# Routing of a top-2-of-8 expert layer: rows normed by products with a diagonal matrix and a row of ones, counts and registers in another order, gates in a function called from the product loop

## The chip, the cores and the metric

The program runs on one core of a Trainium2 chip. The metric is the device time of one execution in microseconds (us), the median of several runs. The core's engines are TensorE (PE in the rows, with its weight loads as PEld), VectorE (DVE), ScalarE (ACT), GpSimd (POOL) and SyncE (SP), each with its own queue of instructions that it works off in order. TensorE's clock has two levels, 1.2 and 2.4 GHz; the rows give the granted clock as a share of the upper one.

## The reference: what is computed

Two layers over 512 latent tokens of width 1024 with a context prefix of 256 tokens. Each layer is a norm, a projection, four groups of mixers, an output projection, and then a norm and a feed-forward part. The change is in the feed-forward part of the second layer, eight experts of which each token uses two:

```
h      = rms_norm(x) modulated: h = (x * rstd) * A + B, A and B vectors over the 1024 channels
logits = h @ router                       # 512 x 8
top 2 experts of each token; gates = softmax over the two logits
y      = sum over the two of gate * (silu(h @ w1) * (h @ w3)) @ w2     # 1408 hidden units per expert
out    = rms_norm(x + g2 * y)
```

All operands are float32.

## The kernel before, in words

Products with weights are made in three passes (`mm3`, lines 272 to 274): each operand is split into a high and a low part that the array multiplies exactly, the high part by a ScalarE copy (L259), the low part by a VectorE subtraction (L260). `load_split` issues the load of a weight tile on SP's queue into a tile named `raw...` and then splits it into `hi...` and `lo...`.

`moe_x` turns each of the eight channel tiles of the residual so that tokens are on partitions, and leaves `x A` in `hm`, a tile of 128 partitions by 4 blocks of 1024 channels. `moe_route` then does the following, in this order of the text:

- It sums the squares on TensorE (L1658) and takes `rs`, the reciprocal root mean square (tile `mrs`), and the logits `lg` of each token.
- It norms the rows: ScalarE multiplies each block of `hm` by `rs` (L1671), GpSimd adds `B` (tile `Br`) to three of the four blocks (L1673), VectorE to the last one (L1700). Four DMAs on ScalarE's queue write them to a DRAM buffer `hd` (L1702).
- It ranks the eight logits of each token by comparing all pairs on VectorE (`rank`, L1680 to L1684), selects the two best (`one`, `sel`), and computes the gates.
- It counts the tokens of each expert, and each token's position, by eight small products with triangular matrices and matrices of ones (L1708 to L1712), copies both out of the accumulator (`pos`, L1714), and ranks the experts by their counts.
- The numbers of the experts in that order go to `regs` (L1730), which SP loads into registers; the addresses of the weight loads depend on them. Everything else (some 40 small VectorE instructions) leads to `inv` (L1774), the token of every row of the dispatch buffer, which comes out of eight products with one-hot matrices (L1773).

`moe_run` then walks eight runs of experts: three of two blocks of 128 rows and five of one block, in two lanes that take turns. GpSimd's queue gathers the rows of a block from `hd` by `inv` (`xr`, L1799), TensorE turns them (L1812), ScalarE and VectorE split them (`xh`, `xl`). For each of eleven tiles of hidden units of a run two loads (`rawm`, three buffers) and one (`rawv`, two buffers) come in; the first product goes into `sml`, then Silu (`mt`, L1840), then the second product into `y`.

The order in which the instructions of an engine stand is not that of the text: a scheduler writes it out ahead of the run from the dependences, and the engines keep to it. Tiles that are allocated in the pool `mh` (of the routing) give their room to tiles of the product loop; tiles in `mo` live to the end.

Of the kernel before, what the change touches and what calls it, by code (L numbers as in the profile page):

```python
# [23 lines left out]
T = LAT + CTX  # L24
# [10 lines left out]
# columns of the per-layer parameter block  # L35
# [4 lines left out]
# columns of the constant block  # L40
# [7 lines left out]
def _consts():  # L48
    """Constants that depend on shapes alone."""
# [54 lines left out]
def _col_tiles():  # L104
    """Column tiles (lists of w_in columns) that are computed channels x tokens, and the token-major group."""
# [17 lines left out]
# heads 0, 2, 1, 3  # L123
# [6 lines left out]
def _pack(inp):  # L130
# [7 lines left out]
    # shifts and scales of two channel tiles side by side  # L138
# [84 lines left out]
class Ker:  # L223
# [19 lines left out]
    def weave(*gens):  # L243
        """Traces several streams side by side: (generator, steps at a time)."""
# [31 lines left out]
    def gemm_col(s, ps, parts, act, segs):  # L276
        """ps[:, tokens] = weights^T act for one tile of 128 output channels.  parts: (first k, tiles) of the weights."""
# [53 lines left out]
    def seg_gemm(s, lhsT, rhs, ntok, use, tag=None):  # L331
        """use(columns, psum) for each segment of lhsT^T rhs; lists of operands are summed."""
# [46 lines left out]
    def setup_masks(s):  # L379
        """The constants that the recurrences need."""  # L380
# [7 lines left out]
        # masks of the pairs that hold the diagonal as well  # L388
# [31 lines left out]
    def ada_rest(s, tp, room):  # L420
        """The first layer's second half and the second layer, a channel tile at a time, without the tensor engine.
        s.adaw(): where the weights of a tile go."""
# [4 lines left out]
        for n in range(72):  # L427
# [4 lines left out]
            # the second layer's context goes no further than its keys  # L432
# [12 lines left out]
    def sumsq(s, m, n, pool, x=None, eng=None):  # L445
        """Adds the squares of channel tile m of the residual to s.acc."""
# [31 lines left out]
    def norm(s, l, mod, sh, sc, gcol, wp, rs, hhi, hlo, ks, ts=None):  # L478
        """Channel tiles ks of the normalised and modulated residual in two parts; ts: room for two tiles."""
# [18 lines left out]
    def proj(s, l, cols, eng=None):  # L498
        """Column tiles (number, tokens) of the input projection into PSUM (channels x tokens); several at once go k by k."""
# [4 lines left out]
    def proj_tok(s, l, it, vt):  # L504
        """HGRN inputs and window values, tokens on partitions."""
# [39 lines left out]
    def rw_prep(s, l, last, g, tp):  # L545
        """Everything of the RWKV mixer that needs no state."""
# [34 lines left out]
        # values, centred over the channels of their head, tokens on partitions  # L581
# [9 lines left out]
        # bonus: (sum over the head of r k r_k) v  # L591
# [17 lines left out]
    def flip(s, out, lhs, rhs, start=True, stop=True):  # L609
        """out[half j] = lhs(j)^T rhs(j) for both j; the array's column halves work side by side."""  # L610
# [11 lines left out]
    def rw_first(s, last, g, tp):  # L622
        """The first operands of the first direction, ahead of the rest."""
# [43 lines left out]
        # the chain of a pair beside the operands of the next  # L667
# [17 lines left out]
    def rw_pair(s, d, lo, last, g, tp, z):  # L685
        """Operands and triangular inverses of two neighbouring chunks of one direction."""
# [34 lines left out]
        # G^T = [-beta|kappa]^T [alpha|rho], masked  # L721
# [9 lines left out]
        # (I + L)^-1 by doubling.  T: the inverses (TU, padded TP), TT: their transposes  # L731
# [15 lines left out]
        # kappa and -beta, tokens on partitions  # L747
# [12 lines left out]
        for i in range(1, 6):  # L760
# [4 lines left out]
            def half(x):  # L765
                # the columns of the earlier half of every block
# [28 lines left out]
    def rw_chain(s, d, lo, ch, last, g, O, done, tp, z, ops, Z, final):  # L795
        """One chunk of the state recurrence; returns the state after it."""
# [44 lines left out]
    def head_squares(s, O, i, a, b, sq):  # L841
        """Sums of squares of the heads of chunks a .. b of recurrence i's output."""
# [3 lines left out]
    def head_rms(s, last):  # L846
        """Their reciprocal root means."""
# [41 lines left out]
    def hg_gates(s, l, z, key, tp, tmp):  # L889
        """log decays (cumulated within the chunks, in z) and keys of both directions."""  # L890
# [25 lines left out]
        # log max(f, 1e-30) as the sum of two logarithms whose arguments stay in the range of the function  # L916
# [11 lines left out]
    def hgrn(s, last, q, b, key, it, O, tp):  # L928
        """The recurrences of both directions, in segments of four chunks."""
# [13 lines left out]
        def padded(dst, f, sel, engs):  # L943
            """dst[half, c, t, half, sel] = f(half)"""
# [4 lines left out]
        for d in range(2):  # L949
# [3 lines left out]
            for sg in ((2, 1, 0) if d else (2, 0, 1)):  # L953
# [3 lines left out]
                # keys scaled to the end of their chunk, tokens on partitions  # L957
# [1013 lines left out]
```

## Time and profile before

| | us |
|---|---|
| median of 3 runs | 2638.28 |
| lowest and highest run | 2634.31, 2647.7 |
| span of the profiled execution, first to last instruction | 2644.5 |
| TensorE busy in the span | 2408.1 |
| VectorE busy | 1660.6 |
| ScalarE busy | 1227.3 |
| GpSimd busy | 484.9 |

The page gives the profiled execution only its span. Of the three runs only the one of 2647.7 us is longer than that span, by 3.2 us, so this is the one that the span fits into, and 3.2 us would lie around it. Times in rows are counted from the span's start. The last products of the layer's output projection end at about 2019 us, the routing follows, and the product loop of the experts runs from about 2050 to about 2602 us.

### The profile page before, as it was taken

To read this page: it belongs to the slowest core of one execution; us is meant where nothing else is said; L and a number is where in the kernel's file an instruction comes from. 1 tells how busy PE (TensorE), PEld (TensorE's weight loads), DVE (VectorE), ACT (ScalarE), POOL (GpSimd) and SP (SyncE) were. 2 spreads that over 40 slices of the span, in tenths; PEclk is the share of its full clock that TensorE was granted. 3 is DMA by queue.
4 is the path that set the end of the run, shared out by engine and by line. 5 is a ranking of instruction groups with operands and counts; after the bars stand their busy time and mean duration, and the time that the engine had idled before them with its cause. 6 is when DMAs were issued, how large, how long until landed. Compare 5 with 4: busy or idle time off the path is not lost. (4 is left out here: it accounts for less than half of the span.)

```text
span 2644.5 us, 46379 instructions
## 1 busy us (share of the span) xinstructions
PE 2408.1 (91%) x18131; PEld 1998.6 (76%) x18131; DVE 1660.6 (63%) x3055; ACT 1227.3 (46%) x2331; POOL 484.9 (18%) x613
## 2 busy tenths in 40 slices
PE   6999788879998999999999997888996999999994
PEld 3889666656586888888888786666674898899993
DVE  5573598777578644344336746876745667667765
ACT  4373356546723211211234654664653556555653
POOL 1010464441011000000020005654102000000002
PEclk9999899989998999999999998998998899999997
DMA  6223110111053433334322130001113888888885
GB/s 245 65 89 111 49 34 20 30 65 57 1 178 129 144 112 120 117 116 132 118 81 64 57 116 13 20 16 49 56 36 107 267 270 270 280 265 264 260 277 179
DMA packets 161026, 322.46 MB, mean 122 GB/s; under 512 B 12288, under 2 KB 84736, under 8 KB 160800
## 3 DMA queue, kind: packets, MB, share of 16 engines
q1 hardware_dynamic: 153744, 293.60, 34.2%
q0 software_dynamic: 6480, 23.73, 2.5%
q8 instruction: 144, 2.36, 0.4%
q10 hardware_dynamic: 576, 2.10, 0.2%
q14 instruction: 82, 0.67, 0.1%
HBM read 295.39 MB, written 22.54 MB: 120 GB/s over the span
## 5 line engine op out<-in xcount | busy, mean ns | idle before, releaser
L272 PE MATMUL big<-hhi,hiw 128*128 128x512 f32 (+1 forms) x1504 | 520.8, 347 | 9.1 <-ACT hhi L491 4.6
L273 PE MATMUL big<-hlo,hiw 128*128 128x512 f32 (+1 forms) x1504 | 523.6, 348 | 2.4 <-DVE hlo L492 2.4
L274 PE MATMUL big<-hhi,low 128*128 128x512 f32 (+1 forms) x1504 | 519.5, 346 | 5.8 <-DVE low L260 3.9
L259 ACT CAST hiw<-raww 128x512 fp32r<-128x512 f32 (+3 forms) x208 | 158.4, 769 | 616.9 <-PE big L273 413.4
L272 PEld LDWEIGHTS big<-hhi,hiw 128*128 128x128 f32 x1504 | 286.2, 191 | 53.2 <-ACT hhi L491 5.7
L274 PEld LDWEIGHTS big<-hhi,low 128*128 128x128 f32 x1504 | 286.2, 190 | 45.1 <-DVE low L260 5.6
L273 PEld LDWEIGHTS big<-hlo,hiw 128*128 128x128 f32 x1504 | 286.4, 190 | 41.0 <-DVE hlo L492 4.2
L260 DVE TENSOR_TENSOR lom<-rawm,him 128x1024 fp32r<-128x1024 f32 x176 | 215.1, 1225 | 128.0 <-ACT him L259 126.7
L260 DVE TENSOR_TENSOR low<-raww,hiw 128x512 fp32r<-128x512 f32 (+3 forms) x196 | 177.3, 909 | 161.1 <-ACT hiw L259 160.8
L259 ACT CAST him<-rawm 128x1024 fp32r<-128x1024 f32 x176 | 184.3, 1047 | 150.4 <-PE sml L273 60.7
L272 PE MATMUL sml<-xh,him 128*128 128x256 f32 x528 | 152.0, 288 | 0.0
L273 PE MATMUL sml<-xl,him 128*128 128x256 f32 x528 | 149.5, 283 | 0.0
L274 PE MATMUL sml<-xh,lom 128*128 128x256 f32 x528 | 149.4, 283 | 0.0
L260 DVE TENSOR_TENSOR lov<-rawv,hiv 128x1024 fp32r<-128x1024 f32 x88 | 107.5, 1222 | 38.2 <-ACT hiv L259 37.8
L272 PE MATMUL sml<-him,xh 128*128 128x256 f32 x440 | 127.4, 290 | 0.7 <-DVE xl L260 0.6
L273 PE MATMUL sml<-lom,xh 128*128 128x256 f32 x440 | 125.4, 285 | 0.0
L274 PE MATMUL sml<-him,xl 128*128 128x256 f32 x440 | 125.3, 285 | 0.0
L273 PE MATMUL big<-gl,hiw 128*128 128x512 f32 (+1 forms) x352 | 119.5, 339 | 0.0
L272 PE MATMUL big<-gh,hiw 128*128 128x512 f32 (+1 forms) x352 | 118.9, 338 | 0.0
L274 PE MATMUL big<-gh,low 128*128 128x512 f32 (+1 forms) x352 | 118.2, 336 | 0.0
L259 ACT CAST hiv<-rawv 128x1024 fp32r<-128x1024 f32 x88 | 92.4, 1050 | 51.3 <-PE y L274 41.5
L757 POOL TENSOR_TENSOR Gm<-G,mskf 128x256 f32<-128x256 f32 x120 | 99.5, 836 | 85.7 <-PE a L612 82.5
(560 smaller groups left out, 5633.7 us busy)
## 6 DMA issues: line engine op xcount, KB each, us to landing
rawm<-in_m SPq DMA_DIRECT2D x176, 512.0 KB, 5.1
rawv<-in_m SPq DMA_DIRECT2D x88, 512.0 KB, 4.7
raww<-in_wadt SPq DMA_DIRECT2D x56, 512.0 KB, 3.5
raww<-in_w SPq DMA_DIRECT2D x52, 512.0 KB, 3.9
raww<-in_winc SPq DMA_DIRECT2D x92, 256.0 KB, 2.8
raww<-in_wout SPq DMA_DIRECT2D x16, 512.0 KB, 4.1
wadt<-in_wadt SPq DMA_DIRECT2D x16, 512.0 KB, 4.4
raww<-in_w SPq DMA_DIRECT2D x16, 448.0 KB, 3.3
```

Source lines behind the costliest of these rows:

```text
L259: s.S.copy(hi, src)
L260: (eng or s.V).tensor_sub(lo, src, hi)
L272: s.E.matmul(out, ah, bh, start=start, stop=False)
L273: s.E.matmul(out, ah, bl, start=False, stop=False)
L274: s.E.matmul(out, al, bh, start=False, stop=stop)
L757: P.tensor_mul(x, G[:, :, 0, :, 0], s.mskf[:, 1 - d, i][:, None, None].to_broadcast(sh))
```

## The change

It edits `moe_route`, moves part of it into a new function `moe_tables`, and passes that function to `moe_run`, which calls it behind its third step.

- **Rows.** For each of the four blocks of `hm` ScalarE writes a diagonal matrix `dg` (the unit matrix with each row scaled by `rs`). For each half of 512 columns TensorE multiplies `hm` by it and adds, by a product of a row of ones with `Br`, the vector B to each token's row, in an accumulator `ph` of the three buffers `tx`; ScalarE copies that back to `hm`. The block's DMA to `hd` follows. The operands are plain float32.
- **Selection and counts.** `sel` is one comparison of the rank with 2. The products that count the tokens come ahead of those that give positions and have an accumulator of their own; only they are copied out (`cnt`), and positions are read from the accumulator later.
- **Registers.** `regs` is computed directly behind the ranks of the counts in the text.
- **Gates.** The gates and the cast of the row numbers (`rows`) are written in `moe_tables`.
- Several small tiles and `ohp` (the one-hot matrices) move from the pool `mh` to the pool `mo`.

Comments were taken out as well; the diff leaves those lines out.

```diff
         for j in range(4):
-            S.activation(s.hm[:, j], s.hm[:, j], AF.Copy, scale=rs[:, j:j + 1])
-            if j < 3:
-                P.tensor_add(s.hm[:, j], s.hm[:, j], s.Br)
+            dg = tp.tile([128, 128], F32, name="dg", bufs=2)
+            S.activation(dg, s.idn, AF.Copy, scale=rs[:, j:j + 1])
+            for q in range(2):
+                c = slice(512 * q, 512 * q + 512)
+                ph = s.tx()
+                E.matmul(ph, dg, s.hm[:, j, c], start=True, stop=False)
+                E.matmul(ph, s.ones[0:1], s.Br[0:1, c], start=False, stop=True)
+                S.copy(s.hm[:, j, c], ph)
+            S.dma_start(s.hd[128 * j:128 * j + 128], s.hm[:, j])
...
-        V.tensor_add(sel, one[0], one[1])
...
-        V.tensor_add(s.hm[:, 3], s.hm[:, 3], s.Br)
-        for j in range(4):
-            S.dma_start(s.hd[128 * j:128 * j + 128], s.hm[:, j])
...
+        V.tensor_single_scalar(sel, rk, 2.0, op=OP.is_lt)
+
+        ps, pq = s.tx(), s.tx()
         sf = sel.rearrange("p a b -> p (a b)")
+        for d in range(4):
+            E.matmul(pq[:, :8], s.onr, sf[:, 8 * d:8 * d + 8], start=d == 0, stop=d == 3)
         E.matmul(ps[:, :32], s.ltr, sf, start=True, stop=False)
...
-        pos = tp.tile([128, 5, 8], F32, name="pos")
-        V.tensor_copy(pos, ps[:, :40].rearrange("p (a b) -> p a b", a=5))
...
+        cnt = s.mo.tile([128, 1, 8], F32, name="cnt")
+        V.tensor_copy(cnt[:, 0], pq[:, :8])
...
+    def moe_tables(s):
+
+        V, S, tp = s.V, s.S, s.mo
+        lg, one, rf = s.tab
+        V.tensor_copy(s.rows, rf)
...
+        V.reciprocal(s.gates[:, 0], v[:, 0])
+        V.tensor_mul(s.gates[:, 1], s.gates[:, 0], v[:, 1])
...
             prev = (run, f, *cur)
+            if at == 2 and tables:
+                tables()
```

What the scheduler makes of it shows at three places; elsewhere the order of the product loop is the same, instruction by instruction.

On TensorE, from the logits to the first gathered rows, before (L1708 to L1712 are the counts and positions, L1773 gives `inv`, L1812 turns the gathered rows):

```order
L1666 MATMUL tx<-cst,lgs 128x8 x4
L1708 MATMUL tx<-sel,ltr 128x32
L1710 MATMUL tx<-sel,onr 128x24
L1710 MATMUL tx<-sel,onr 128x16
L1710 MATMUL tx<-sel,onr 128x8
L1712 MATMUL tx<-sel,onr 128x8 x4
L1773 MATMUL tx<-ohb,ohp 128x16 x8
L1812 MATMUL sml<-cst,xr 128x128 x8
```

and now (the pair L1677, L1678 stands eight times; L1700 is the counts):

```order
L1666 MATMUL tx<-cst,lgs 128x8 x4
L1677 MATMUL tx<-hm,dg 128x512
L1678 MATMUL tx<-Br,cst 128x512
...
L1700 MATMUL tx<-sel,onr 128x8 x4
L1701 MATMUL tx<-sel,ltr 128x32
L1703 MATMUL tx<-sel,onr 128x24
L1703 MATMUL tx<-sel,onr 128x16
L1703 MATMUL tx<-sel,onr 128x8
L1766 MATMUL tx<-ohb,ohp 128x16 x8
L1823 MATMUL sml<-cst,xr 128x128 x8
```

All sixteen products of the rows stand ahead of the counts, and the counts have moved ahead of the positions.

On VectorE, at the end of the routing, before (`ohp`, `ohb` are the one-hot operands of L1773, L260 splits the first weight tiles):

```order
L1769 TENSOR_TENSOR ohp<-pl,mcst 128x512
L1766 TENSOR_TENSOR ohb<-ge,mcst 128x64 x2
L1769 TENSOR_TENSOR ohp<-pl,mcst 128x512
L1774 CAST inv<-tx 128x15
L260 TENSOR_TENSOR lom<-rawm,him 128x1024 x2
L260 TENSOR_TENSOR lov<-rawv,hiv 128x1024
```

and now:

```order
L1763 TENSOR_TENSOR ohp<-pl,mcst 128x512
L1759 TENSOR_TENSOR ohb<-ge,mcst 128x64 x2
L1763 TENSOR_TENSOR ohp<-pl,mcst 128x512
L260 TENSOR_TENSOR lom<-rawm,him 128x1024
L1767 CAST inv<-tx 128x15
L260 TENSOR_TENSOR lom<-rawm,him 128x1024
L260 TENSOR_TENSOR lov<-rawv,hiv 128x1024
```

The low part of the first weight tile has moved ahead of the cast that makes `inv`.

On ScalarE, at the start of the product loop, before (`him`, `hiv` are high parts of weights, `xh` of the gathered rows):

```order
L259 CAST him<-rawm 128x1024 x2
L259 CAST hiv<-rawv 128x1024
L259 CAST him<-rawm 128x1024
L259 CAST xh_19380<-sml 128x512 x2
L259 CAST hiv<-rawv 128x1024
L259 CAST him<-rawm 128x1024
```

and now:

```order
L259 CAST him<-rawm 128x1024 x2
L259 CAST hiv<-rawv 128x1024
L259 CAST him<-rawm 128x1024
L259 CAST xh_19403<-sml 128x512
L259 CAST hiv<-rawv 128x1024
L259 CAST xh_19403<-sml 128x512
L259 CAST him<-rawm 128x1024
```

The second half of the first block's rows now stands behind the second `rawv` tile.

## Rows read from the trace of the kernel before

**Rows 1.** Head of the profile page.

```profile
span 2644.5 us, 46379 instructions
```

**Rows 2.** Busy time by stretch: PE, PEld, DVE, ACT, POOL, clock, DMA share, GB/s.

```profile
2023.00:2026.00 3.00, 0.00 (x0) 0.00 (x0) 2.79 (x6) 3.00 (x6) 1.46 (x1) 1.00 0.00 0
2026.00:2032.00 6.00, 0.00 (x0) 0.00 (x0) 5.93 (x7) 2.85 (x3) 5.75 (x3) 0.51 0.00 0
...
2061.00:2066.00 5.00, 4.04 (x16) 3.03 (x16) 2.81 (x4) 2.25 (x5) 0.95 (x1) 0.50 0.63 179
...
2068.00:2600.00 532.00, 523.37 (x3678) 484.08 (x3677) 369.60 (x460) 315.71 (x445) 13.84 (x21) 1.00 0.81 264
```

**Rows 3.** Instructions in order of time: start, us, engine, line, idle before.

```profile
2023.27 4.30 ACT L1671 ACTIVATE hm<-hm,mrs 128x1024 f32<-128x1024 f32 x4
...
2024.54 7.21 POOL L1673 TENSOR_TENSOR hm<-hm,Br 128x1024 f32<-128x1024 f32 x3 [9.60 <-ACT hm L1671]
2024.78 2.45 DVE L1683 TENSOR_TENSOR acc<-acc 128x256 f32<-128x256 f32 x1
2027.27 0.42 DVE L1684 TENSOR_REDUCE rk<-acc 128x32 f32<-128x256 f32 x1
...
2029.50 2.30 DVE L1693 TENSOR_TENSOR tt<-lg,one 128x32 f32<-128x32 f32 x1
...
2032.05 0.37 PE L1708 MATMUL tx<-sel,ltr 128*128 128x32 f32 x1 [9.25 <-DVE v L1694]
...
2033.93 0.20 DVE L1714 COPY pos<-tx 128x40 f32<-128x40 f32 x1 [1.46 <-PE tx L1712]
```

**Rows 4.** The same view, from the counts to the first gather.

```profile
2035.49 1.22 DVE L1700 TENSOR_TENSOR hm<-hm,Br 128x1024 f32<-128x1024 f32 x1
...
2037.33 0.15 DVE L1730 CAST regs<-ef 1x8 int32<-1x8 f32 x1
...
2039.35 0.91 SPq L264 DMA_DIRECT2D rawm<-in_m  x2
...
2044.02 2.20 ACT L259 CAST him<-rawm 128x1024 fp32r<-128x1024 f32 x2 [9.58 <-PE tx L1773]
2044.03 0.17 DVE L1774 CAST inv<-tx 128x15 int32<-128x15 f32 x1 [1.29 <-PE tx L1773]
2045.03 1.07 POOL L1799 DMA_INDIRECT xr<-hd,inv  x1 [13.28 <-DMA rawm<-in_m]
2045.10 2.38 DVE L260 TENSOR_TENSOR lom<-rawm,him 128x1024 fp32r<-128x1024 f32 x2 [0.90 <-ACT him L259]
...
2047.13 0.51 SPq L264 DMA_DIRECT2D rawv<-in_m  x1
```

**Rows 5.** Landing of the DMAs issued in 2039.3 to 2039.5, 2045 to 2045.2, 2047 to 2047.5.

```profile
rawm<-in_m SPq DMA_DIRECT2D x1, 512.0 KB, 4.5
xr<-hd,inv POOLq DMA_INDIRECT x1, 4.5
rawv<-in_m SPq DMA_DIRECT2D x1, 512.0 KB, 9.8
```

**Rows 6.** Instructions in order of time, start of the product loop.

```profile
2049.82 1.94 PE L1812 MATMUL sml<-cst,xr 128*128 128x128 f32 x8 [5.83 <-ACT him L259]
...
2052.36 0.58 PE L272 MATMUL sml<-him,xh 128*128 128x256 f32 x1 [0.59 <-DVE xl L260]
...
2056.99 1.05 ACT L259 CAST hiv<-rawv 128x1024 fp32r<-128x1024 f32 x1 [4.60 <-DMA rawv<-in_m]
...
2060.29 0.28 ACT L1840 ACTIVATE mt<-sml 128x128 f32<-128x128 f32 x1
...
2061.82 1.11 PE L1812 MATMUL sml<-cst,xr 128*128 128x128 f32 x4 [0.41 <-DVE xl L260]
```

**Rows 7.** TensorE in order of time, a float32 product of 512 columns.

```profile
630.30 1.02 PE L1256 MATMUL sc<-k,q 128*128 128x512 f32 x2
631.16 0.31 PE L1102 MATMUL pt<-cst,pe 128*128 128x128 f32 x1
```

More of the change, by code (lines that the diff above doesn't have):

```diff
@@ L1608, in moe_begin @@
         s.rt = mh.tile([128, KT, 8], F32, name="router")
-        s.mc = mh.tile([128, 349], F32, name="mcst")
+        s.mc = s.mo.tile([128, 349], F32, name="mcst")
         s.Q.dma_start(s.rt, s.I['router'])
@@ L1652, in moe_route @@
         E, V, S, P, tp = s.E, s.V, s.S, s.P, s.mh
-        mc, rows, gates, regs = s.mc, s.rows, s.gates, s.regs
+        mc, regs = s.mc, s.regs
         tri, iota = mc[:, :64].rearrange("p (a b) -> p a b", a=8), mc[:, 64:72]
@@ L1666, in moe_route @@
             E.transpose(ps[:, 8 * j:8 * j + 8], lgs[:, 128 * j:128 * j + 128], s.idn[:8, :8])
-        lg = tp.tile([128, 4, 8], F32, name="lg")
+        lg = s.mo.tile([128, 4, 8], F32, name="lg")
         V.tensor_mul(lg, ps[:, :32].rearrange("p (a b) -> p a b", a=4), rs[:, :, None].to_broadcast([128, 4, 8]))
@@ L1684, in rank @@
             V.tensor_reduce(dst, gt, AX.X, OP.add)
-        rk = tp.tile([128, 4, 8], F32, name="rk")
+        rk = s.mo.tile([128, 4, 8], F32, name="rk")
         rank(rk, lg, 4)
-        one = [tp.tile([128, 4, 8], F32, name=f"one{i}") for i in range(2)]
         sel = tp.tile([128, 4, 8], F32R, name="sel")
-        t = tp.tile([128, 4, 8], F32, name="tt")
-        v = tp.tile([128, 2, 4], F32, name="v12")
-        for i in range(2):
-            V.tensor_single_scalar(one[i], rk, float(i), op=OP.is_equal)
-            V.tensor_mul(t, lg, one[i])
-            V.tensor_reduce(v[:, i], t, AX.X, OP.add)
-        V.tensor_add(sel, one[0], one[1])
-        V.tensor_sub(v[:, 1], v[:, 1], v[:, 0])
-        S.activation(v[:, 1], v[:, 1], AF.Exp)
-        V.tensor_scalar_add(v[:, 0], v[:, 1], 1.0)
-        V.tensor_add(s.hm[:, 3], s.hm[:, 3], s.Br)
-        for j in range(4):
-            S.dma_start(s.hd[128 * j:128 * j + 128], s.hm[:, j])
-        V.reciprocal(gates[:, 0], v[:, 0])
-        V.tensor_mul(gates[:, 1], gates[:, 0], v[:, 1])
-        ps = s.tx()
+        V.tensor_single_scalar(sel, rk, 2.0, op=OP.is_lt)
+        ps, pq = s.tx(), s.tx()
         sf = sel.rearrange("p a b -> p (a b)")
+        for d in range(4):
+            E.matmul(pq[:, :8], s.onr, sf[:, 8 * d:8 * d + 8], start=d == 0, stop=d == 3)
         E.matmul(ps[:, :32], s.ltr, sf, start=True, stop=False)
@@ L1710, in moe_route @@
             E.matmul(ps[:, 8 * d:32], s.onr, sf[:, :32 - 8 * d], start=False, stop=d == 3)
-        for d in range(4):
-            E.matmul(ps[:, 32:40], s.onr, sf[:, 8 * d:8 * d + 8], start=d == 0, stop=d == 3)
-        pos = tp.tile([128, 5, 8], F32, name="pos")
-        V.tensor_copy(pos, ps[:, :40].rearrange("p (a b) -> p a b", a=5))
-        cnt = pos[:, 4:5]
-        er = tp.tile([128, 1, 8], F32, name="er")
-        rank(er, cnt, 1)
-        w = tp.tile([128, 8, 8], F32, name="ew")
-        nb, big, base, cap, ov, ob, u = (w[:, i] for i in range(7))
-        V.tensor_single_scalar(nb, cnt[:, 0], 0.0, op=OP.is_gt)
-        for j in range(1, 4):
-            V.tensor_single_scalar(u, cnt[:, 0], 128.0 * j, op=OP.is_gt)
-            V.tensor_add(nb, nb, u)
+        cnt = s.mo.tile([128, 1, 8], F32, name="cnt")
+        V.tensor_copy(cnt[:, 0], pq[:, :8])
+        er = s.mo.tile([128, 1, 8], F32, name="er")
+        rank(er, cnt, 1)
         ef = tp.tile([128, 13], F32, name="ef")
@@ L1730, in moe_route @@
         V.tensor_copy(regs, ef[0:1, :8])
+        w = s.mo.tile([128, 8, 8], F32, name="ew")
+        nb, big, base, cap, ov, ob, u = (w[:, i] for i in range(7))
+        V.tensor_single_scalar(nb, cnt[:, 0], 0.0, op=OP.is_gt)
+        for j in range(1, 4):
+            V.tensor_single_scalar(u, cnt[:, 0], 128.0 * j, op=OP.is_gt)
+            V.tensor_add(nb, nb, u)
         V.tensor_single_scalar(big, er[:, 0], 3.0, op=OP.is_lt)
@@ L1744, in moe_route @@
         V.tensor_sub(u, u, base)
-        pp = pos[:, :4]
+        pp = ps[:, :32].rearrange("p (a b) -> p a b", a=4)
         sh = [128, 4, 8]
+        t = tp.tile([128, 4, 8], F32, name="tt")
         V.tensor_tensor(t, pp, cap[:, None].to_broadcast(sh), OP.is_ge)
@@ L1750, in moe_route @@
         V.tensor_tensor(t, t, base[:, None].to_broadcast(sh), OP.add)
-        rf = tp.tile([128, 2, 4], F32, name="rf")
+        rf = s.mo.tile([128, 2, 4], F32, name="rf")
+        one = [s.mo.tile([128, 4, 8], F32, name=f"one{i}") for i in range(2)]
+        y = tp.tile([128, 4, 8], F32, name="yy")
         for i in range(2):
-            V.tensor_mul(one[i], one[i], t)
-            V.tensor_reduce(rf[:, i], one[i], AX.X, OP.add)
-        V.tensor_copy(rows, rf)
+            V.tensor_single_scalar(one[i], rk, float(i), op=OP.is_equal)
+            V.tensor_mul(y, one[i], t)
+            V.tensor_reduce(rf[:, i], y, AX.X, OP.add)
         rr = rf.rearrange("p a b -> p (a b)")
-        ge = tp.tile([128, 8, 17], F32, name="ge")
+        ge = s.mo.tile([128, 8, 17], F32, name="ge")
         V.tensor_tensor(ge, rr[:, :, None].to_broadcast([128, 8, 17]), mc[:, None, 200:217].to_broadcast([128, 8, 17]), OP.is_ge)
-        pl = tp.tile([128, 8], F32, name="pl")
+        pl = s.mo.tile([128, 8], F32, name="pl")
         V.tensor_reduce(pl, ge[:, :, 1:], AX.X, OP.add)
@@ L1766, in moe_route @@
             V.tensor_mul(ohb[:, 4 * i:4 * i + 4], ge[:, 4 * i:4 * i + 4, :16], mc[:, 345:349][:, :, None].to_broadcast([128, 4, 16]))
-        ohp = tp.tile([128, 8, 128], F32R, name="ohp")
+        ohp = s.mo.tile([128, 8, 128], F32R, name="ohp")
+        place = mc[:, None, 217:345].to_broadcast([128, 4, 128])
         for i in range(2):
-            V.tensor_tensor(ohp[:, 4 * i:4 * i + 4], pl[:, 4 * i:4 * i + 4, None].to_broadcast([128, 4, 128]),
-                            mc[:, None, 217:345].to_broadcast([128, 4, 128]), OP.is_equal)
-        ps = s.tx()
+            V.tensor_tensor(ohp[:, 4 * i:4 * i + 4], pl[:, 4 * i:4 * i + 4, None].to_broadcast([128, 4, 128]), place, OP.is_equal)
+        pi = s.tx()
         for i in range(8):
-            E.matmul(ps[:, :16], ohp[:, i], ohb[:, i], start=i == 0, stop=i == 7)
-        V.tensor_copy(s.inv, ps[:, :15])
+            E.matmul(pi[:, :16], ohp[:, i], ohb[:, i], start=i == 0, stop=i == 7)
+        V.tensor_copy(s.inv, pi[:, :15])
         V.tensor_add(u, ob, ov)
@@ L1786, in moe_route, with moe_run @@
         V.tensor_copy(s.regv, ef[0:1, 8:13])
-    def moe_run(s, lanes, wp):
+        s.tab = lg, one, rf
+    def moe_tables(s):
+        V, S, tp = s.V, s.S, s.mo
+        lg, one, rf = s.tab
+        V.tensor_copy(s.rows, rf)
+        y = tp.tile([128, 4, 8], F32, name="yl")
+        v = tp.tile([128, 2, 4], F32, name="v12")
+        for i in range(2):
+            V.tensor_mul(y, lg, one[i])
+            V.tensor_reduce(v[:, i], y, AX.X, OP.add)
+        V.tensor_sub(v[:, 1], v[:, 1], v[:, 0])
+        S.activation(v[:, 1], v[:, 1], AF.Exp)
+        V.tensor_scalar_add(v[:, 0], v[:, 1], 1.0)
+        V.reciprocal(s.gates[:, 0], v[:, 0])
+        V.tensor_mul(s.gates[:, 1], s.gates[:, 0], v[:, 1])
+    def moe_run(s, lanes, wp, tables=None):
         E, V, S, P = s.E, s.V, s.S, s.P
@@ L1905, in moe @@
                 with s.pool("mw") as wp:
-                    s.moe_run([[(expert(j), [2 * j, 2 * j + 1]) for j in range(3)], [(expert(j), [3 + j]) for j in range(3, 8)]], wp)
+                    s.moe_run([[(expert(j), [2 * j, 2 * j + 1]) for j in range(3)], [(expert(j), [3 + j]) for j in range(3, 8)]], wp, s.moe_tables)
                 nov = s.nc.values_load(s.regv[0:1, 4:5], min_val=0, max_val=s.NOV)
```

## The prediction

> **What bounds the kernel now.** I read the table of stretches first, because it tells where a delay survives. From 2068 us to 2600 us, the product loop of the experts, TensorE is busy 523.37 of 532 us at clock 1.00 [rows 2]: it is the bound there, almost without a gap, and every microsecond by which the loop starts later or earlier comes out at the end. Before 2068 us it is the other way round: from 2023 to 2032 us TensorE has nothing to do at all [rows 2], and the order of time shows what it waits for. The ranking on VectorE is held up: L1683 takes 2.45 us and L1693 takes 2.30 us, while L1684, a reduction over the 256 columns that L1683 writes, takes 0.42 us between them [rows 3]. Both long ones run while GpSimd adds B (L1673, from 2024.54 us on for 7.21 us) and end about when one of its three additions ends. So some 4 us of VectorE's time in these two are a hold by GpSimd, and the counts (L1708) can start only at 2032.05 us [rows 3].
>
> The Trainium skill, "SBUF — State Buffer", section "Who interferes with whom", says that a VectorE instruction with two inputs in SBUF and a GpSimd instruction that reads SBUF exclude each other for the whole instruction, and that a reduction does not take part. The three rows agree. By that rule alone, dropping the additions would give those 4 us back to the ranking; whether they reach the end depends on what TensorE does in that time.
>
> From the counts on the chain is: `pos` at 2033.93 us, `regs` at 2037.33 us, first weight load issued at 2039.35 us, `inv` at 2044.03 us, first gather at 2045.03 us [rows 3, 4], 4.5 us to its landing [rows 5], transposes at 2049.82 us, first product at 2052.36 us [rows 6].
>
> **The change part by part.**
>
> *Products of the rows (L1677, L1678).* Sixteen float32 products of 512 columns. Such a product shows as two instructions, and two of them took from 630.30 to 631.16 us, 0.86 us [rows 7], at full clock. Sixteen are 16 x 0.86 = 13.8 us. A diagonal matrix is an eighth of an L1671 in width, so between 4.30 / 4 / 8 = 0.13 us and 4.30 / 4 = 1.08 us [rows 3]; I take 0.3, since its 128 columns are nearest to the small end. ScalarE is free for it at 2023.27 us, where L1671 started. The products then run from 2023.6 to 2037.4 us. ScalarE's part hides below them: per block two copies, each half an L1671 or 0.55 us, a matrix of 0.3 us and the issue of a DMA, against 3.4 us of products. The bounds of this term: the product with the row of ones has only one row of weights, no row here shows such a shape, and if every product went as a single instruction it would be 16 x 0.43 = 6.9 us; at clock 0.50 it would be 27.5 us.
>
> The Trainium skill, "TensorE: Matmul & The Clock Gate", section "Why this matters for your kernels", has it that a product over 32 rows takes as long as one over all 128. By that rule the row of ones is as dear as the diagonal matrix, and the sum would be the 13.8 us that I take.
>
> *What waits behind them.* TensorE works in order, and the order puts the counts (L1700) behind all sixteen. `sel` will be ready at about 2026 us, as GpSimd no longer holds VectorE, and it helps nothing: the gain on VectorE goes into a wait for TensorE. Eight products at clock 0.50 took from 2032.05 to 2033.93 us; four at full clock are a quarter of that, 0.5 us. So `cnt` comes at 2037.4 + 0.2 for the last product's tail (1.02 less 0.86 us [rows 7]) + 0.5 = 2038.1 us, against `pos` at 2033.93: **+4.1 us**.
>
> *From the counts to the registers.* Before 3.40 us. The addition L1700 (1.22 us [rows 4]) is gone from between, and one small instruction net, 0.1 us. That leaves 2.1 us: `regs` at 2040.2 us, the first weight load 2.0 us later as before, at 2042.2 us, landing 4.5 us later [rows 5] at 2046.7 us: **+2.8 us**. The row DMAs, spread from 2028 us on, now leave less in front of it; I count nothing for that.
>
> *From the counts to the gather.* Before 10.10 us; less 1.2 for L1700 and 0.4 for four gate instructions, `inv` could come at 2046.6 us. But the order puts the first `lom` ahead of `inv`, and it needs the first weight tile: landing at 2046.7, `him` 1.1 us, `lom` 1.2 us (halves of 2.20 and 2.38 [rows 4]), so `inv` goes at about 2049.1 us: **+5.1 us**. The gather, the transposes and the first product move by the same, to 2050.1, 2054.9 and 2057.45 us.
>
> *Where it is given back.* The first run's 24 products of 256 columns take 24 x 256 / 1.2 GHz = 5.1 us at the lower clock and end at about 2062.6 us. Before, they were not what came last: the second `rawv` landed 9.8 us after its issue [rows 4, 5], its cast (L259, 2056.99 us) stood ahead of the Silu on ScalarE, and the Silu came at 2060.29 us [rows 6]. Now the Silu waits for the products instead: 2062.6, **+2.3 us**. The transposes of the other lane's rows (L1812 at 2061.82 us) need a first set of four transposes (estimated at 0.7 us, between the 1.11 us of L1812 x4 and half of it), a cast and a subtraction of 512 columns (half of 1.1 and of 1.2 us) behind those products, and come at about 2064.9 us, +3.1 us. Against that, before, TensorE stood at clock 0.50 from 2061 to 2066 us with 4.04 us of work [rows 2], after a pause behind the products. That pause goes, as ScalarE no longer holds the Silu back. If the clock, once up, stays up, up to 2.0 us come back: a net of +1.1 to +3.1 us. I take **+2 us**.
>
> *Gates, rows, smaller pieces.* The order puts the gates and `one` ahead of `cnt` on VectorE and not into the loop: they lie under the wait for TensorE and cost nothing; without that cover they would be some ten instructions of 0.1 us. Their exponential sits between two copies on ScalarE, which by the sum above has over 1 us to spare per block. The tiles moved to `mo` only change which waits the first casts carry: the first `him` now waits for row DMAs, issued by 2038.5 us, well ahead of its weights. The rest of the loop is in the same order.
>
> *Sum.* The profiled span of 2644.5 us [rows 1] becomes 2646.5 us, with 3.2 us around it 2649.7 us against 2647.7. That execution is the slowest of the three; on the median of 2638.28 the same 2 us give 2640.3 us. About 0.5%, 13.2 us, is what a measurement of this kernel can tell from no change, as its runs lie 13.4 us apart: I forecast no change that can be told.
>
> **The rivals.**
>
> *The clock falls under the products (slower).* TensorE's clock was 1.00 until 2026 us and then fell, after 3 us without an instruction; it stays low until products come close together [rows 2]. If the light work of 2019 to 2023 us makes it fall in the first products, the sixteen take up to 27.5 us instead of 13.8, and the delay grows one for one, as everything hangs behind them: +2 + 13.7 us, 2654.0 us. It decides (over 13.2 us) only if the clock is low for four fifths of the products. Against it: the pause between L1666 and the first product is under 1 us, and float32 work elsewhere runs at full clock [rows 7].
>
> *The products are cheap.* At 6.9 us they end at 2030.5 us, `cnt` comes 2.8 us ahead of `pos`, the weights land 4 us and `inv` 2 to 4 us earlier: the hold by GpSimd and the L1700 that were removed are a real gain of about 4 us, 2634 us. Against it stands the price of [rows 7].
>
> *The second `rawv` sets the pace.* The order puts half of the first rows' split behind its cast. It is issued 0.8 us after the first `lom`, at 2049.9 us; if it again takes 9.8 us it lands at 2059.7, the second twelve products start at 2061.4 instead of 2060.0 and their last third waits for `xl` as well. That adds some 2 us: 2642.3 us. Against it: by then fewer loads are in flight than at 2047 us.
>
> *The gates part does nothing*, since the order hoists it. This is in my forecast already; the time is the same.
>
> **How the numbers follow.** No change to tell, 2634 to 2646 us around 2640.3: 0.70. The second `rawv` as well: 0.11, also within. Cheap products: 0.06, within. The clock falls: 0.10. Something that the order does not show, either way: 0.03. The median of a few runs carries half of their spread, some 6 us, which lets each case reach over its edge a little: faster by over 0.5% 0.05, within 0.83, slower 0.12. The range runs from the cheap products, 2634 less 1, to just short of the clock's case, 2652: outside lie most of the clock's 0.10 and the tails, no more than 0.2.
>
> **What would show it.** Sixteen pairs at a pitch of 0.43 us per instruction between 2023.6 and 2037.4 us with clock 1.00; VectorE idle some 10 us ahead of `cnt`; no VectorE instruction of 128x256 above 0.5 us; first weight load at about 2042 us; `lom` ahead of `inv`, `inv` near 2049 us; first product near 2057.5 us; the Silu right behind the products; clock 1.00 by about 2062 us; the loop from then on as before. I am wrong if the pitch is 0.86 us (clock), if `cnt` is ahead of 2034 us (price), or if the loop itself, beyond 2070 us, changes its length by several microseconds.

## The result and the profile after

| | median us | runs | ratio to before, 95% interval |
|---|---|---|---|
| before, on the same chip | 2638.96 | 2634.31 to 2647.7 (7) | |
| changed | 2660.28 | 2656.83 to 2795.51 (7) | 1.0077 [1.0059, 1.0094] |
| changed, again | 2664.39 | 2660.34 to 2665.37 (4) | 1.0092 [1.0075, 1.0109] |

The change costs 21 to 26 us, 0.8 to 0.9%, where no change to tell was forecast (2640.3 us, range to 2652). The profile that came with the result is of an execution that was disturbed throughout (2795.51 us); all rows after are those of the repeat. Each ratio below is against the kernel before as timed on the same chip at that time: medians of 2638.82 us (the repeat, the unit matrix, two matrices of ones, rows as before), 2640.82 us (no row of ones, counts first, B behind the gather, the single run of the matrix of ones) and 2639.60 us (the rest). Head of the repeat's page, to be set against [rows 1]:

```profile
span 2662.0 us, 46444 instructions
```

Busy time by stretch, the view of [rows 2] (PE, PEld, DVE, ACT, POOL, clock, DMA share, GB/s):

```profile
2014.00:2018.00 4.00, 3.03 (x12) 1.41 (x12) 3.44 (x13) 1.69 (x8) 0.00 (x0) 1.00 0.00 0
2018.00:2020.00 2.00, 2.00 (x3) 0.51 (x3) 0.75 (x5) 0.83 (x3) 0.00 (x0) 0.52 0.00 0
...
2024.00:2046.00 22.00, 22.00 (x25) 5.57 (x23) 0.00 (x0) 3.69 (x7) 0.00 (x0) 0.50 0.13 53
2046.00:2072.00 26.00, 9.29 (x42) 8.73 (x42) 15.17 (x63) 7.46 (x10) 4.73 (x4) 0.50 0.79 283
2072.00:2074.00 2.00, 1.69 (x12) 1.44 (x10) 1.43 (x2) 1.89 (x3) 0.00 (x0) 0.82 0.00 0
2074.00:2600.00 526.00, 514.00 (x3580) 474.20 (x3580) 361.43 (x450) 308.50 (x436) 16.12 (x23) 0.99 0.82 265
```

Instructions in order of time, which answer to [rows 3, 4, 6]:

```profile
2013.71 0.67 DVE L1647 TENSOR_TENSOR hm<-tx,Ar 128x512 f32<-128x512 f32 x1
...
2015.61 1.12 PE L1677 MATMUL tx<-hm,dg 128*128 128x512 f32 x2 [0.97 <-ACT dg L1673]
...
2016.62 0.42 DVE L1690 TENSOR_TENSOR acc<-acc 128x256 f32<-128x256 f32 x1
2016.66 1.12 PE L1678 MATMUL tx<-Br,cst 1*128 1x512 f32 x2
...
2041.42 2.08 PE L1677 MATMUL tx<-hm,dg 128*128 128x512 f32 x2
...
2043.43 2.07 PE L1678 MATMUL tx<-Br,cst 1*128 1x512 f32 x2
2045.43 1.02 PE L1700 MATMUL tx<-sel,onr 128*128 128x8 f32 x4
...
2046.48 0.17 DVE L1705 COPY cnt<-tx 128x8 f32<-128x8 f32 x1 [24.40 <-PE tx L1700]
...
2048.72 0.15 DVE L1714 CAST regs<-ef 1x8 int32<-1x8 f32 x1
...
2050.39 0.91 SPq L264 DMA_DIRECT2D rawm<-in_m  x2
...
2055.57 1.22 DVE L260 TENSOR_TENSOR lom<-rawm,him 128x1024 fp32r<-128x1024 f32 x1 [1.34 <-ACT him L259]
...
2056.72 0.17 DVE L1767 CAST inv<-tx 128x15 int32<-128x15 f32 x1
...
2057.80 1.30 POOL L1810 DMA_INDIRECT xr<-hd,inv  x1 [51.01 <-DMA rawv<-in_m]
...
2065.34 1.94 PE L1823 MATMUL sml<-cst,xr 128*128 128x128 f32 x8 [9.91 <-issue]
...
2073.20 0.28 ACT L1851 ACTIVATE mt<-sml 128x128 f32<-128x128 f32 x1
```

Landing of the DMAs issued in 2050.3 to 2050.5 and in 2057.7 to 2057.9 (compare [rows 5]):

```profile
rawm<-in_m SPq DMA_DIRECT2D x1, 512.0 KB, 4.1
...
xr<-hd,inv POOLq DMA_INDIRECT x1, 7.2
```

Three things are to be seen. The ranking is no longer held: the comparison that took 2.45 us [rows 3] takes 0.42 us (L1690). VectorE then waits 24.40 us for the counts. And the sixteen products that it waits for run from 2015.61 to 2045.43 us, 29.8 us, TensorE busy all the time, but from about 2018 us on at clock 0.50, the 1.2 GHz level. (The profile models the ends of products, so "busy" is by its records.) A product went from a pitch of 1.05 us (2015.61 to 2016.66) to 2.01 us (2041.42 to 2043.43).

The part of the program ahead of the routing differs by 8.2 us between these two profiled executions and by up to 12.3 us among all of them, so I count from the last L1647, the last instruction of `moe_x`. Before, it stood here:

```profile
2021.87 0.67 DVE L1647 TENSOR_TENSOR hm<-tx,Ar 128x512 f32<-128x512 f32 x1
```

From there to the end of the span it was 2644.5 - 2021.87 = 622.6 us, and is now 2662.0 - 2013.71 = 648.3 us: +25.7 us, which the timed runs bear out. Behind that point profiles still differ by a few us (with the rows as before the end is 4.9 us earlier than before, the timed medians differ by 1.1 us). The loss starts at the products:

| us behind the last L1647 | `cnt` or `pos` | `inv` | gathered rows turned | end |
|---|---|---|---|---|
| before | 12.1 | 22.2 | 28.0 | 622.6 |
| changed (repeat) | 32.8 | 43.0 | 51.6 | 648.3 |
| unit matrix for the row of ones | 16.3 | 26.4 | 35.5 | 627.9 |
| two matrices of ones | 15.3 | 25.6 | 34.9 | 626.6 |
| 32 rows | 19.4 | 29.5 | 38.1 | 630.3 |
| 64 rows | 19.4 | 29.7 | 38.4 | 630.0 |
| matrix of ones first, row of ones second | 24.4 | 34.7 | 43.8 | 635.1 |
| the same, again | 30.3 | 40.4 | 49.8 | 642.0 |
| counts first, unit matrix | 5.2 | 22.2 | 33.6 | 624.3 |
| no row of ones | 10.7 | 20.9 | 30.0 | 620.3 |
| rows as before | 9.9 | 20.2 | 27.2 | 617.7 |
| B behind the gather | 4.8 | 13.9 | 19.8 | 616.7 |

### The profile page after: what moved, and what is told of

It is laid out like the page before. It is cut to its first block, busy times and chain, and to the rows that moved or that the text cites. A ratio compares the mean times of both kernels' runs of the same rounds, so it can differ in the third digit from the quotient of the medians.

```text
span 2793.3 us, 46444 instructions
## 1 busy us (share of the span) xinstructions
PE 2587.9 (93%) x18163; PEld 2089.4 (75%) x18163; DVE 1663.2 (60%) x3054; ACT 1231.8 (44%) x2339; POOL 474.5 (17%) x610
## 3 DMA queue, kind: packets, MB, share of 16 engines
q1 hardware_dynamic: 153744, 293.60, 32.8%
## 5 line engine op out<-in xcount | busy, mean ns | idle before, releaser
L272 PE MATMUL big<-hhi,hiw 128*128 128x512 f32 (+1 forms) x1504 | 543.9, 363 | 8.3 <-ACT hhi L491 4.1
L273 PE MATMUL big<-hlo,hiw 128*128 128x512 f32 (+1 forms) x1504 | 547.4, 364 | 2.2 <-DVE hlo L492 2.2
L274 PE MATMUL big<-hhi,low 128*128 128x512 f32 (+1 forms) x1504 | 545.0, 363 | 0.8 <-POOL low L260 0.8
L272 PEld LDWEIGHTS big<-hhi,hiw 128*128 128x128 f32 x1504 | 293.2, 195 | 63.4 <-issue 5.5
L274 PEld LDWEIGHTS big<-hhi,low 128*128 128x128 f32 x1504 | 291.9, 194 | 47.9 <-issue 1.9
L260 DVE TENSOR_TENSOR lom<-rawm,him 128x1024 fp32r<-128x1024 f32 x176 | 215.3, 1225 | 141.2 <-ACT him L259 140.7
L260 DVE TENSOR_TENSOR low<-raww,hiw 128x512 fp32r<-128x512 f32 (+3 forms) x196 | 177.3, 909 | 186.4 <-ACT hiw L259 185.5
L260 DVE TENSOR_TENSOR lov<-rawv,hiv 128x1024 fp32r<-128x1024 f32 x88 | 107.8, 1225 | 48.6 <-ACT hiv L259 47.1
L273 PE MATMUL big<-gl,hiw 128*128 128x512 f32 (+1 forms) x352 | 125.8, 357 | 0.0
L274 PE MATMUL big<-gh,low 128*128 128x512 f32 (+1 forms) x352 | 125.0, 355 | 0.0
```

The lines of the kernel that those rows point to most:

```text
L260: (eng or s.V).tensor_sub(lo, src, hi)
L272: s.E.matmul(out, ah, bh, start=start, stop=False)
L273: s.E.matmul(out, ah, bl, start=False, stop=False)
L274: s.E.matmul(out, al, bh, start=False, stop=stop)
```

## The experiments

The theory after the result: the product over a single row of weights does not hold TensorE's clock up, and the lower clock under the products, not their number or their place in the order, makes the loss. The rivals: the products are too long at any clock; or something else in the change (gates, order, pools) costs the time.

**The changed kernel again.**

> The changed kernel once more, for a profile at full clock outside the routing. It should take about 2660 us, 21 us over the kernel before. Theory (the clock): TensorE's granted clock falls to 0.50 in the first of the sixteen pairs of products and stays there, so a product takes about 1.7 us and all sixteen about 27 us; cnt comes some 18 us later than pos did. Rival (the price alone): clock 1.00, products of 0.86 us, and the 21 us are lost elsewhere, in the product loop.

Measured: 2664.39 us; its rows are those above. The clock falls in the third product, about 2.4 us after the first one starts.

**A unit matrix for the row of ones.** `Br` holds B on all 128 partitions, so the second product can use all rows, with the same result.

```diff
-                E.matmul(ph, s.ones[0:1], s.Br[0:1, c], start=False, stop=True)
+                E.matmul(ph, s.idn, s.Br[:, c], start=False, stop=True)
```

> B is added by a product of the unit matrix with Br, which holds B on all 128 partitions, instead of a row of ones with one row of Br: the same sixteen products and the same result, but all of them over 128 rows. Theory A (a product over a single row does not keep the clock up): clock 1.00 in the products, sixteen in about 14 us, time about 2646 us, 14 under the changed kernel. Theory B (zeros: diagonal and unit matrices do not keep it up): no different from the changed kernel, 2660 us. Theory C (float32 products at this place do not keep it up, whatever they hold): 2660 us.

Measured: 2642.92 us (2639.11 to 2647.89), ratio 1.0014 [1.0004, 1.0024]. Its stretches and then its order of time:

```profile
2016.00:2018.00 2.00, 2.00 (x6) 0.80 (x6) 1.79 (x10) 0.78 (x2) 0.00 (x0) 1.00 0.00 0
...
2026.00:2028.00 2.00, 2.00 (x6) 0.92 (x5) 0.00 (x0) 0.64 (x2) 0.00 (x0) 1.00 0.56 227
```

```profile
2014.86 1.12 PE L1677 MATMUL tx<-hm,dg 128*128 128x512 f32 x2 [0.97 <-ACT dg L1673]
...
2026.98 1.02 PE L1677 MATMUL tx<-hm,dg 128*128 128x512 f32 x2
2027.84 1.02 PE L1678 MATMUL tx<-Br,cst 128*128 128x512 f32 x2
...
2029.24 0.17 DVE L1705 COPY cnt<-tx 128x8 f32<-128x8 f32 x1 [8.90 <-PE tx L1700]
```

As many products, in the same order, with as many non-zero weights (one in each column): the clock stays at 1.00, the pitch is 0.86 us, and some 21 us of the loss are gone. That refutes both rivals as the cause of the large loss. The light work ahead of the products is the same in both kernels, so it does not bring the clock down by itself.

**Two matrices of ones** (the norm is left out).

```diff
-                E.matmul(ph, dg, s.hm[:, j, c], start=True, stop=False)
-                E.matmul(ph, s.ones[0:1], s.Br[0:1, c], start=False, stop=True)
+                E.matmul(ph, s.ones, s.hm[:, j, c], start=True, stop=False)
+                E.matmul(ph, s.ones, s.Br[:, c], start=False, stop=True)
```

> Both products of a pair have the matrix of ones as weights, 128 rows without a zero; the normed rows are then sums over tokens, so this leaves out the norm and the output is another. Same number, shape and order of products. Theory A (single row): clock 1.00, about 2646 us, like the unit matrix. Theory B (zeros): clock 1.00 here, about 2646 us, but not with the unit matrix. Theory C (float32): clock 0.50 here too, 2660 us.

Measured: 2644.14 us, ratio 1.002 [1.001, 1.0031], clock 1.00: whether the weights are mostly zeros makes no difference once all rows are used.

**Rows as before**, the rest of the change kept (ScalarE scales, GpSimd and VectorE add B, four DMAs behind `sel`).

> Only the rest of the change: the rows are normed as before, by ScalarE, GpSimd and one VectorE addition, with their DMAs behind the selection; selection, counts, registers and gates are as changed. My sum: the gates' four small instructions and the second accumulator's copy leave the path, some 0.5 to 1 us, and sel no longer waits for two masks and an addition that GpSimd holds up, up to 2 us. So 2636 to 2639 us, 0 to 3 us under the kernel before. Rival (the reordered small parts cost by themselves, for instance through lom ahead of inv): 2641 us or more.

Measured: 2637.77 us, ratio 0.9995 [0.9986, 1.0005]. The rest of the change costs nothing that can be told, and the hold by GpSimd is back, now also on `sel`. Order of time:

```profile
2015.65 7.21 POOL L1674 TENSOR_TENSOR hm<-hm,Br 128x1024 f32<-128x1024 f32 x3 [9.60 <-ACT hm L1672]
2015.89 2.45 DVE L1684 TENSOR_TENSOR acc<-acc 128x256 f32<-128x256 f32 x1
...
2018.83 1.75 DVE L1689 TENSOR_SCALAR sel<-rk 128x32 fp32r<-128x32 f32 x1
```

**No row of ones.** The second product is left out, and so is B.

> The changed kernel without the product of the row of ones, so B is left out of the rows and the output is another: eight products with diagonal matrices instead of sixteen products. Theory A (only the single-row product takes the clock down): clock 1.00, eight products in 6.9 us, cnt 2.8 us ahead of where pos stood, time about 2635 us, 7 under the run with the unit matrix. Theory B (diagonal matrices take it down too, as they are mostly zeros): clock 0.50, eight products in about 14 us, time like the run with the unit matrix, 2643 us.

Measured: 2637.89 us, ratio 1.0001 [0.9985, 1.0018], clock 1.00 in all eight diagonal products, so diagonal matrices alone do not bring it down. `cnt` comes 1.4 us earlier than `pos` did, not the 2.8 us expected. Eight products cost nothing that the unheld ranking does not give back.

**Counts first.** The unit matrix again, and the loop of the rows moved behind the products of the counts and positions, ahead of the copy to `cnt`.

> The unit matrix as in the run before, and the sixteen products written behind the counts and positions, so that TensorE's order has L1700 to L1703 ahead of them. Theory (what is left of the loss at full clock is the wait of the counts behind the products): cnt some 5 us behind the last hm of moe_x instead of 16, first weight load 9.5 us behind it instead of 20; but the rows then reach hd some 24 us behind it, so the gather comes at 24 instead of 27 us, and the time is about 2639 us, 3 to 4 under the run with the unit matrix. Rival (the counts' place does not matter, the loss is in the gather's landing): 2643 us.

Measured: 2643.27 us (2638.26 to 2648.14), ratio 1.0008 [0.9993, 1.0024], not the 2639 us of the theory: no gain over the unit matrix alone that the timed runs can tell, though `cnt` comes 11 us earlier. Order of time:

```profile
2020.94 0.15 DVE L1714 CAST regs<-ef 1x8 int32<-1x8 f32 x1
...
2035.40 0.33 ACTq L1702 DMA_DIRECT2D hd<-hm  x1
2035.58 0.17 DVE L1767 CAST inv<-tx 128x15 int32<-128x15 f32 x1 [1.44 <-PE tx L1766]
...
2042.31 1.07 POOL L1810 DMA_INDIRECT xr<-hd,inv  x1 [35.83 <-issue]
```

The products of `inv` stand behind the sixteen, and the last DMA of the rows is issued only at 2035.40 us, while the weights are already loading. The gather starts 6.7 us behind `inv` instead of 1.0 [rows 4], 28.9 us behind the last L1647 where 24 was expected. Landing of the DMAs issued in 2035.3 to 2035.5:

```profile
hd<-hm ACTq DMA_DIRECT2D x1, 512.0 KB, 5.8
```

The last DMA of the rows so lands at about 2041.2 us, and the gather starts 1.1 us later, so this DMA is what it waits for. The wait has moved from the counts to the rows. The rival's time came, but not for its reason: the gather lands after 4.4 us here.

**B behind the gather.** No products: ScalarE scales a block, its DMA follows at once, and VectorE adds B, now a value per partition, to the gathered and turned rows.

```diff
+        s.Bc = s.mo.tile([128, KT], F32, name="Bc")
+        V.tensor_copy(s.Bc, mod[:, 24:32, 0])
...
+            S.activation(s.hm[:, j], s.hm[:, j], AF.Copy, scale=rs[:, j:j + 1])
             S.dma_start(s.hd[128 * j:128 * j + 128], s.hm[:, j])
...
-                    s.split(a[o], c[o], pv)
+                    xf = wp.tile([128, 4, 128], F32, name="xf", bufs=2)
+                    V.tensor_tensor(xf, pv, s.Bc[:, 4 * q:4 * q + 4][:, :, None].to_broadcast([128, 4, 128]), OP.add)
+                    s.split(a[o], c[o], xf)
```

> A version meant to beat both: no products of the rows at all and no addition on GpSimd; ScalarE scales the rows as before and sends each block at once; B is added on VectorE to the gathered and turned rows, one addition of 512 columns per half block, ahead of their split. The rest is as changed. Theory (TensorE's queue and GpSimd's hold on VectorE are what cost): no VectorE instruction of the ranking is held, cnt 5 us behind the last hm of moe_x (before 12), inv some 6 to 7 us earlier than before, time about 2632 us, 6 to 7 under the kernel before. Rival (the start of the loop is bound by its loads, or the 22 added additions delay the splits): 2638 us or more.

Measured: 2632.09 us (2627.14 to 2637.0), ratio 0.9966 [0.9954, 0.9979], as expected (2632): 0.3% faster than before, and faster than the changed kernel. Order of time (its last L1649 line, the marker, is at 2017.91 us):

```profile
2022.68 0.17 DVE L1700 COPY cnt<-tx 128x8 f32<-128x8 f32 x1 [0.45 <-PE tx L1695]
...
2031.80 0.17 DVE L1762 CAST inv<-tx 128x15 int32<-128x15 f32 x1 [1.25 <-PE tx L1761]
...
2038.79 0.69 DVE L1822 TENSOR_TENSOR xf<-sml,Bc 128x512 f32<-128x512 f32 x1 [0.64 <-PE sml L1818]
```

Here the ranking is unheld and nothing stands ahead of the counts: `inv` comes 8.3 us earlier than before and the end 5.9 us. Of the 8.2 us at the turned rows 6.7 are left at the first Silu; the additions (0.69 us for half a block) stand between, but what they take back was not measured alone.

**A matrix of ones first, the row of ones second** (the norm is left out): a single run first, then seven.

> The first product of each pair has the matrix of ones as weights instead of the diagonal matrix, the second is the single row as changed; the rows are sums over tokens, so the norm is left out and the output is another. Theory A (the single row does it by itself): the clock falls to 0.50 in the products, and the time is about 2660 us. Theory D (it takes both, the zeros of the diagonal and the single row): clock 1.00, about 2645 us.

> The same kernel as in the one look with a matrix of ones as the first product's weights and the single row as the second's (the norm is left out). If the clock falls whenever half of the products use a single row of weights, and the matrix of ones only lets it fall some us later than the diagonal matrix does, the clock is at 0.50 again before the products end and the time is about 2651 us (2648 to 2655). If the late fall of the look was chance, the times scatter between 2645 us (no fall) and 2662 us (fall at the start).

Measured: 2651.09 us in the single run, between the two values expected; then 2655.64 us (2648.41 to 2663.12, 7 runs), ratio 1.0059 [1.0036, 1.0082]. TensorE in order of time, in the single run and in the profile of the later one:

```profile
2024.54 1.12 PE L1678 MATMUL tx<-Br,cst 1*128 1x512 f32 x2
2025.59 1.91 PE L1677 MATMUL tx<-hm,cst 128*128 128x512 f32 x2
```

```profile
2015.55 1.13 PE L1678 MATMUL tx<-Br,cst 1*128 1x512 f32 x2
2016.61 2.08 PE L1677 MATMUL tx<-hm,cst 128*128 128x512 f32 x2
```

The clock falls in both, without a pause, but once in the eleventh product and once in the fifth, and the times scatter accordingly. These two profiles and that of the changed kernel come from three chips. So the fall comes with the single rows, and its moment differs between executions of one kernel. Whether the matrix of ones puts it off stays open: these products also start without the 0.97 us pause that the changed kernel has.

**32 and 64 rows.** B through rows of weights that are all 1/32 or 1/64, with the same result.

```diff
+        on = tp.tile([32, 128], F32, name="on")
+        V.memset(on, 1.0 / 32)
...
-                E.matmul(ph, s.ones[0:1], s.Br[0:1, c], start=False, stop=True)
+                E.matmul(ph, on, s.Br[0:32, c], start=False, stop=True)
```

> The second product takes B through 32 rows of weights that are all 1/32, with the same result. If a product counts for the clock only when it fills the array's rows (my theory), 32 of 128 rows are a quarter, the clock falls as with one row, perhaps some us later, and the time is 2655 to 2664 us. If it is something about a single row alone (one partition read), the clock stays at 1.00 and the time is that with the unit matrix, 2643 us.

> The same with 64 rows of weights that are all 1/64. If the rows in use count in proportion, this lies between one row (2664 us) and 128 rows (2643 us): a fall late in the products or none, 2643 to 2655 us. If every product that is not over the full 128 rows counts as none, 2660 to 2664 us. If only the single row is special, 2643 us and clock 1.00 in all products.

Measured: 2649.06 us (2645.64 to 2667.22, 10 runs), 1.004 [1.0017, 1.0062], and 2647.22 us (2641.07 to 2660.26, 10 runs), 1.0031 [1.001, 1.0052]. A stretch with 32 rows and then TensorE's order of time:

```profile
2028.00:2030.00 2.00, 2.00 (x5) 0.59 (x4) 0.00 (x0) 0.59 (x1) 0.00 (x0) 1.00 0.07 27
```

```profile
2015.70 1.12 PE L1679 MATMUL tx<-hm,dg 128*128 128x512 f32 x2 [0.97 <-ACT dg L1675]
...
2030.45 1.12 PE L1679 MATMUL tx<-hm,dg 128*128 128x512 f32 x2
2031.50 1.12 PE L1680 MATMUL tx<-Br,on 32*128 32x512 f32 x2
2032.56 0.61 PE L1702 MATMUL tx<-sel,onr 128*128 128x8 f32 x4
```

The clock holds at 1.00 through all products in both profiles, so my theory that only full rows count fell. Whether it is the single row alone stays open: with 32 rows two of ten runs took 2662.37 and 2667.22 us, with 64 rows two took 2659.69 and 2660.26 us, about as long as the changed kernel. Their mean clocks (0.959, 0.960, 0.961 and 0.964) lie in the range of the changed kernel's runs of 2657 to 2671 us (0.958 to 0.965), but so do some of the shorter runs (0.964 and 0.965 at 2653 to 2656 us). None of the four has a trace, so a fall in them is a guess. And the pitch is 1.05 us here (15 pitches from 2015.70 to 2031.50 us), 16.9 us for sixteen, against 0.865 and 13.8 us with the unit matrix (2014.86 to 2027.84 us): some 3 us of the loss come without any fall of the clock, and the longer pitch did not by itself bring the clock down in these two profiles. The weight loads (PEld) show where the pitch may come from, in the changed kernel and then with the unit matrix:

```profile
2016.66 0.29 PEld L1678 LDWEIGHTS tx<-Br,cst 1*128 1x128 f32 x2 [0.76 <-issue]
2016.66 1.12 PE L1678 MATMUL tx<-Br,cst 1*128 1x512 f32 x2
```

```profile
2015.40 0.19 PEld L1678 LDWEIGHTS tx<-Br,cst 128*128 128x128 f32 x1 [0.24 <-issue]
2015.83 1.02 PE L1678 MATMUL tx<-Br,cst 128*128 128x512 f32 x2
```

With 128 rows in both products a load starts 0.43 us ahead of its product; with one row, and likewise with 32 and 64, it starts together with it. The pitch differs by 0.19 us, which is what one load takes. That the one causes the other is read from these rows and not tested.

## Why the prediction was wrong

The step that failed is the one on the clock: *float32 work elsewhere runs at full clock*, taken from a product over 128 rows [rows 7] and carried over to pairs of which one has a single row. The text had named this shape as one that no row shows, but asked only how long it takes, not what it does to the clock. The rival *the clock falls under the products* was the case that came, at 0.10 and with the wrong doubt: it took the light work ahead as the cause, whereas the clock was 1.00 until 2018 us and fell inside the products, and with the same light work ahead the unit matrix kept it at 1.00.

Its price, +15.7 us and 2654.0 us, was too low as well. At the lower clock a product takes 2.0 us, not 2 x 0.86, as the pitch of mixed pairs is already 1.05 us at full clock: the sixteen take 29.8 us where it had 27.5. The gather's first rows land after 7.2 us instead of 4.5 [rows 5], among weight loads that now start at the same time; but of the 23.7 us by which the rows are turned later, 21.1 are left at the first Silu and 19.8 at the third. And in the profiled execution the loop loses some 4 us more at a later run's start (the Silu at 2221.44 us is 19.6 us behind its counterpart of before, that at 2281.72 us 23.7), where the clock falls once more; stretches of the changed kernel:

```profile
2224.00:2226.00 2.00, 0.73 (x2) 0.30 (x2) 2.00 (x3) 0.76 (x3) 0.00 (x0) 1.00 0.83 234
2226.00:2228.00 2.00, 1.79 (x9) 1.79 (x10) 0.41 (x3) 0.59 (x1) 0.44 (x1) 0.58 0.93 282
```

Before, the clock stays at 1.00 there. The unit matrix's profile has such a fall too (0.50 from 2210 to 2212 us, with 1.1 us of loss), and in the two profiles of the matrix of ones with the row of ones the Silu's delay stays within 1.2 us from its third to its last (11.8 and 17.9 us at the third). So these last us are not shown to come from the products; why the pause is longer is not settled.

Point by point:

- *Sixteen products, 13.8 us.* 29.8 us. With 128 rows in both products 13.8: the price was right for the shape that it was taken from. In pairs with 32 rows sixteen take 16.9 us at full clock, so a part of the price was wrong whatever the clock did. The upper bound of 27.5 us did not hold the value.
- *Counts behind the products, +4.1 us.* +20.7; with the unit matrix 16.3 - 12.1 = +4.2. The order was read rightly.
- *Counts to registers 2.1 us, registers to first load 2.0, landing 4.5.* 2.24, 1.67 and 4.1 us.
- *`lom` ahead of `inv`, `inv` 11.0 us behind `cnt`.* The order is as said; 10.2 us. The lower clock adds nothing here, since TensorE waits for VectorE.
- *Gather by as much as `inv`.* No: +23.7 against +20.8, the 7.2 us of landing. With the unit matrix likewise, +7.6 against +4.2.
- *Given back in the loop.* The Silu does come right behind the products; but with the unit matrix the first Silu is +4.9 us and the third +3.5, not +2, with the gather's rows landing 7.8 us after its issue instead of 4.5; later runs of experts, one of them with such a fall of the clock, bring the end to +5.3. One sum was off as well: 2062.6 + 0.7 + 0.55 + 0.6 makes 2064.45 us for the other lane's transposes, not 2064.9, so +2.6 and not +3.1; it does not change the +2 by half a us.
- *The hold by GpSimd goes and helps nothing.* Right: 0.42 us, `sel` 3.8 us behind the last L1647 instead of 9.9, and a wait in its place. Rows as before and the eight products show about no change; only with nothing ahead of the counts is it worth something (2632.09 us).
- *Gates cost nothing.* Right (2637.77 us with the rows undone).

With the second product over all rows the forecast (2640.3 us) would have been 2.6 us off, with the products, the order and the counts read rightly and the gather's landing 3.3 us too short.

## What to carry to other kernels

Before work is moved onto TensorE, look at which rows of its weights are used: a bias added by a row of ones looks cheap, and among these float32 products in front of a stage in which everything waited it cost 21 us more here than the same product over all rows. Read a price from a row of the same shape, and ask of a shape that no row shows what it does to the clock as well. What stands ahead of a chain's first link in an in-order queue should be work that this link needs; yet moving the products behind the counts only moved the wait to the rows (2643.27 us). Better than moving the additions from engine to engine was to put them where B is a value per partition.

## What the runs showed of the hardware

- TensorE was busy 22.00 of the 22 us from 2024 to 2046 us and was granted 0.50 all the while. "TensorE: Matmul & The Clock Gate" of the Trainium skill, in "What's actually happening", has the clock set by how busy the engine has been; by the profile's busy time alone these rows do not agree with it. With the rows of weights of every second product raised from 1 to 128 the clock was 1.00; with 32 and 64 it was 1.00 in the one profiled execution of each.
- A float32 product of 512 columns had a pitch of 0.86 us among products over 128 rows, and 1.05 us, at the same clock of 1.00, where every second one was over 1, 32 or 64 rows. The Trainium skill, "TensorE: Matmul & The Clock Gate", section "Why this matters for your kernels", has a product over 32 rows take as long as one over 128. Within these pairs the rows agree, 1.05 us for either; but both products are 0.19 us dearer than among products all over 128 rows, of which that rule says nothing.
- With a matrix of ones and a row of ones in turn, the moment of the fall differs between executions of one kernel: after 10.5 us of products in one, after 4.2 us in another.
